# Hybrid attention and recurrence layer: a re-timed program begin (fewer filler products, x scaled by column halves, other banks for its transposes, three weights cast by POOL)

## The chip, the core and the metric

One core of a Trainium2 chip runs the whole program once. The metric is the device time of that run in microseconds (us). TensorE (PE) multiplies matrices into PSUM banks, VectorE (DVE), ScalarE (ACT) and GpSimd (POOL) do elementwise work, and SyncE (SP) issues nearly all transfers. Each engine executes its own list of instructions strictly in the order in which it was written; an instruction that waits for another engine holds up everything behind it in its list.

## The reference, cut to what matters

One layer over 2048 prompt frames and 64 sample frames of width 1024:

```python
def mixer_layer(x, ln_g, w_in, lb, norm_g, w_out, attn_fn, s0):
    aq, ak, av, ag, hq, hf, hi, hg = split(rms_norm(x, ln_g) @ w_in)     # 1024 -> 4096 columns
    o_a = attn_fn(aq, ak, av) * silu(ag)            # 8 heads x 64, chunks of 64, band of 576 keys
    o_b, S = hgrn2_branch(hq, hf, hi, hg, lb, norm_g, s0)                # 4 heads x 128
    y = x + concatenate([o_a, o_b]) @ w_out
    return y, k, v, S
# hgrn2: f = lb + (1 - lb) * sigmoid(hf), gated linear recurrence; final rms_norm on y
```

`lb` comes from a softmax over two rows of `lb_gamma`, computed once on the chip ("the forget bounds").

## The kernel before, in words

The 2112 frames are worked off in four super-blocks of 512, 576 (with the 64 sample frames), 512 and 512 columns. In each, `x` is normalised, transposed and multiplied with the 32 column tiles of `w_in` (projections j = 0 to 31 of that super-block); each projection feeds a recurrence head or a pair of attention heads. The output projection follows at the end.

**Products in three parts.** Every float32 operand is kept as a rounded part and a remainder (`xh` and `xl`, `w[:, 0]` and `w[:, 1]`), and a projection is 24 products into one accumulator bank: eight `xh` with the high weight, eight `xl` with the high weight, eight `xh` with the low weight. In the first super-block the weights come raw: one engine casts the high part (DVE, but POOL for j = 0), POOL subtracts four quarters to make the low part, and the pair is also written back for later super-blocks. Later super-blocks read the pairs back.

**One tile of x.** `x_tile` takes 128 rows of x: ACT squares and sums them (L369) and makes the reciprocal root mean square `rstd` (L337, L338); DVE multiplies the rows by `rstd` and the gain (L377); PE transposes eight 128x128 pieces, four per PSUM bank (L253); ACT casts each bank to `xh` (L403), and DVE subtracts to make `xl` (L407), which frees the bank. A super-block has two halves of two tiles (256 columns; in the second super-block the second half has a further tile of 64 rows). The projections j = 0 and j = 1 of a super-block, and its last two, go half by half, so that the next super-block's tiles can be made in between.

**Program begin.** SP issues the four x tiles and the first four weights; ACT's queue issues the gain row `gin`, `lbg` (the `lb_gamma` rows) and `gnorm`. PE first multiplies the identity with itself into a spare bank, which has no use for the result (`spinning`, L1953: the fillers), spreads the gain row over 128 partitions with two products whose weight has a single row (L1964), and then runs fillers until the planner lets the first transposes go. The forget bounds run behind the transposes of the second half.

**What sets the order.** A planner (`Plan`) in the host code writes out all lists: each piece of work is a generator that says when it wants to go on, by the planner's own clock `C.now` and assumed lengths; PE's list drives the clock. So a change of one length or wait at the start can move rows of every list further down.

Of the kernel before, what the change touches and what calls it, by code (L numbers as in the profile page):

```python
# [17 lines left out]
P = 128  # L18
D = 1024
# [164 lines left out]
def hymba_step(  # L184
# [105 lines left out]
    def forget_bounds():  # L290

        yield lambda: x_there.get((0, 1, 1), (0, 0))[0] == 4
        lmx = T(cst, [P, NHB], F32, "lmx")
        le = T(cst, [P, 2, NHB], F32, "le")
        dve.tensor_tensor(lmx, lbg[:, 0], lbg[:, 1], ALU.max)
        for i in range(2):
            dve.tensor_sub(le[:, i], lbg[:, i], lmx)
        t = C.dve(300)
        yield "A", t
        act.activation(le, le, AF.Exp)  # L300
        t = C.act(8, t)
        yield "D", t
        dve.tensor_add(lmx, le[:, 0], le[:, 1])
        dve.reciprocal(lmx, lmx)
        dve.tensor_mul(lb, le[:, 0], lmx)
        dve.tensor_scalar(oml, lb, -1.0, 1.0, ALU.mult, ALU.add)
        C.dve(400, t)
        have.add("bounds")
# [43 lines left out]
    def x_tile(sb, half, c, here=None, gain=None):  # L352
# [24 lines left out]
        dve.scalar_tensor_tensor(xn[:rows], xn[:rows], r[:rows], g, ALU.mult, ALU.mult)  # L377
        t = C.dve(1070, t)
        yield lambda: x_left.get((sb - 1, half), False)
        yield t  # L380
        ends = []
        for k0 in (0, 4):
            tags = ("g", "tr") if sb else ("acc", "tr", "g", "pv")
            while not any(tk[x].n for x in tags):
                some = [tk[x].when() for x in tags]
                yield min(some) if min(some) < NEVER else C.now + 150.0
            tag = [x for x in tags if tk[x].n][0]
            tk[tag].take()
            pt = psum(tag, bufs={"g": 1, "pv": 1}.get(tag, 2))
            for kt in range(k0, k0 + 4):  # L390
                transpose(pt[:, (kt - k0) * P : (kt - k0) * P + rows], xn[:rows, kt * P : (kt + 1) * P],
                          ident[:rows, :rows])
            ends.append((k0, tag, pt, C.pe()))
            if k0 and here is None:
                tk["xn"].put(1, C.pe())
            C.spawn(x_split(sb, half, c, rows, *ends[-1]), 0 if sb or half else -1)

    def x_split(sb, half, c, rows, k0, tag, pt, t):
# [6 lines left out]
        there(sb, half, 0, t)  # L405
# [4 lines left out]
        there(sb, half, 1, t)  # L410

    def there(sb, half, part, t):
        n, last = x_there.get((sb, half, part), (0, 0.0))
        x_there[sb, half, part] = (n + 1, max(last, t))
# [35 lines left out]
    def w_split(j, nt, raw, t, tok):  # L450
# [4 lines left out]
        if j == 0:  # L455
# [73 lines left out]
    def project(j, ranges, evac, close=True, ready=None):  # L529
# [3 lines left out]
        if ready:  # L533
            yield lambda: ready(0)
        for off, bn in ranges:
# [1366 lines left out]
    def program():  # L1902
# [55 lines left out]
        for _ in range(8):  # L1958
            spinning()
            C.now += 330.0  # L1960
# [7 lines left out]
        while tk["acc"].n == 2:  # L1968
            spinning()
            C.now += 224.0  # L1970
# [4 lines left out]
        for sb in range(nsb):  # L1975
# [6 lines left out]
            for u, (kind, g) in enumerate(JOBS[sb]):  # L1982
# [16 lines left out]
                if u in (1, len(JOBS[sb]) - 1):  # L1999
                    for half in range(2):  # L2000
                        yield from project(j - 1, [halves[half]], before, half == 1,
                                           lambda part: x_ready(sb, half, part))
                        yield from project(j, [halves[half]], evac, half == 1,
                                           lambda part: x_ready(sb, half, part))
# [154 lines left out]
```

## Time and profile before

| | |
|---|---|
| three runs | 1254.45, 1257.12, 1257.91 us; median 1257.12 |
| the profiled execution | 1256.82 us, span 1254.6 us (2.2 us lie around the span) |
| PE busy in the span | 1240.9 us (99%) |
| DVE, ACT, POOL busy | 894.6, 684.7, 415.2 us |
| mean granted TensorE clock | 0.996 |

The profile gives the busy time of each engine in any stretch, with the share of full speed that TensorE's clock was granted, lists instructions in order of time with the idle time ahead of them and what ended it, and sums waits by who was waited for. A bracket such as `[0.97 <-DVE xn L377]` is idle time of the engine just before that row, ended by the named instruction.

### The profile page before, as it was taken

Reading aid. Unit: us, or ns where it says so; the run is one execution under the profiler, and the core shown is the slowest. Engines: PE = TensorE matmul, PEld = TensorE weight load, DVE = VectorE, ACT = ScalarE, POOL = GpSimd, SP = SyncE. Lnnn points to the kernel's source line nnn. Section 1 sums busy time; section 2 is a strip of 40 time slices with the busy share of each in tenths; the row PEclk is TensorE's granted clock in tenths of the full one; section 3 lists DMA queues with packets and bytes.
Section 4 is the critical chain, followed back from the end, with each engine's and each line's share of the span. In section 5 each row is a group of like instructions: output and inputs, shape, how many; then the busy total and the mean of one; then the engine's idle time right before and its main releaser. Section 6 shows DMA issues by size and latency. Waiting matters only on the chain. (4 is left out here: it accounts for less than half of the span.)

```text
span 1254.6 us, 21417 instructions
## 1 busy us (share of the span) xinstructions
PE 1240.9 (99%) x7550; PEld 1093.7 (87%) x7550; DVE 894.6 (71%) x1887; ACT 684.7 (55%) x1533; POOL 415.2 (33%) x700
## 2 busy tenths in 40 slices
PE   8999999999999999999999999999999999999997
PEld 8888888999999999998888888988888888888786
DVE  6687879766867678687486667785857476867775
ACT  5354546654656556574465556665655445643443
POOL 6666665111120110201233242134241103474543
PEclk9999999999999999999999999999999999999999
DMA  8987779656555476655777878677666665987431
GB/s 334 311 306 248 279 285 370 212 158 228 178 189 159 145 223 216 193 166 172 252 266 240 299 255 281 227 248 251 219 244 202 222 219 197 342 275 241 136 125 67
DMA packets 137956, 287.94 MB, mean 230 GB/s; under 512 B 35257, under 2 KB 79289, under 8 KB 120186
## 3 DMA queue, kind: packets, MB, share of 16 engines
q1 hardware_dynamic: 137560, 286.58, 67.4%
q8 instruction: 59, 0.97, 0.3%
q14 instruction: 47, 0.39, 0.1%
q10 hardware_dynamic: 290, 0.01, 0.0%
HBM read 195.31 MB, written 92.27 MB: 229 GB/s over the span
## 5 line engine op out<-in xcount | busy, mean ns | idle before, releaser
L249 PE MATMUL acc<-xh,w 128*128 128x512 f32 (+2 forms) x2752 | 566.4, 345 | 0.7 <-ACT xh L403 0.4
L249 PEld LDWEIGHTS acc<-xh,w 128*128 128x128 f32 x2752 | 439.8, 189 | 50.4 <-issue 0.6
L249 PE MATMUL acc<-xl,w 128*128 128x512 f32 (+2 forms) x1376 | 293.4, 345 | 0.3 <-DVE xl L407 0.3
L249 PEld LDWEIGHTS acc<-xl,w 128*128 128x128 f32 x1376 | 220.2, 189 | 25.1 <-DVE xl L407 0.5
L928 ACT ACTIVATE pr<-pr,nm 128x640 f32<-128x640 f32 (+4 forms) x132 | 100.3, 760 | 59.7 <-DVE nm L911 58.8
L940 ACT CAST ph<-tr 128x512 fp32r<-128x512 f32 (+3 forms) x176 | 87.9, 507 | 74.1 <-PE pv L249 47.8
L464 POOL TENSOR_TENSOR w<-wraw,w 128x256 fp32r<-128x256 f32 x120 | 106.6, 914 | 56.9 <-DVE w L459 40.4
L943 DVE TENSOR_TENSOR ph<-tr,ph 128x512 fp32r<-128x512 f32 (+3 forms) x176 | 101.4, 588 | 27.6 <-ACT ph L940 26.8
L911 DVE CUSTOM_DVE_ANT_0 pr<-s,bias 128x640 f32<-128x640 f32 (+4 forms) x128 | 94.2, 736 | 34.8 <-PE s L249 34.1
L249 PE MATMUL pv<-ph,v 128*128 128x256 f32 (+2 forms) x344 | 97.8, 370 | 0.0
L253 PE MATMUL tr<-ident,pr 128*128 128x128 f32 x580 | 89.0, 273 | 1.4 <-DVE sig L634 0.6
L500 POOL TENSOR_TENSOR xn<-wraw,xn 128x256 fp32r<-128x256 f32 x48 | 39.4, 822 | 142.2 <-ACT xn L497 136.4
L982 DVE TENSOR_TENSOR mixa<-mixa,pv 64x256 f32<-64x256 f32 (+1 forms) x144 | 56.8, 395 | 36.0 <-ACT mixa L978 32.7
L1084 POOL TENSOR_TENSOR mixa<-mixa,sga 128x256 f32<-128x256 f32 (+1 forms) x36 | 29.1, 808 | 158.8 <-DVE mixa L982 146.3
L932 DVE TENSOR_SCALAR pr<-pr,sm 128x640 f32<-128x640 f32 (+4 forms) x132 | 76.9, 583 | 4.7
L253 PEld LDWEIGHTS tr<-ident,pr 128*128 128x128 f32 x580 | 69.9, 140 | 10.8 <-DVE sig L634 1.0
L1521 POOL TENSOR_TENSOR k<-ob 128x512 f32<-128x512 f32 (+2 forms) x20 | 18.2, 911 | 180.7 <-ACT ob L1512 161.9
L564 ACT ACTIVATE sig<-acc 128x512 f32<-128x512 f32 (+2 forms) x64 | 32.0, 499 | 64.8 <-PE acc L249 61.7
L249 PEld LDWEIGHTS pv<-ph,v 128*128 128x128 f32 (+1 forms) x344 | 58.4, 189 | 7.1
L978 ACT COPY mixa<-pv 64x256 f32<-64x256 f32 (+1 forms) x72 | 25.1, 349 | 62.3 <-PE pv L249 58.7
L249 PE MATMUL s<-kd,q 128*128 128x320 f32 (+2 forms) x232 | 56.5, 314 | 0.0
L249 PE MATMUL s<-kd,ql 128*128 128x320 f32 (+2 forms) x232 | 55.7, 310 | 0.0
(324 smaller groups left out, 2140.2 us busy)
## 6 DMA issues: line engine op xcount, KB each, us to landing
w<-wd SPq DMA_DIRECT2D x96, 1024.0 KB, 5.6
wd<-w SPq DMA_DIRECT2D x32, 1024.0 KB, 7.7
wraw<-in_w_in_dram SPq DMA_DIRECT2D x30, 512.0 KB, 5.6
wod<-xn SPq DMA_DIRECT2D x28, 512.0 KB, 5.4
xn<-in_x_prompt_dram SPq DMA_DIRECT2D x23, 512.0 KB, 4.6
bias<-biasd SPq DMA_DIRECT2D x24, 320.0 KB, 5.8
carry<-kd SPq DMA_DIRECT2D x12, 512.0 KB, 3.7
carry<-v SPq DMA_DIRECT2D x12, 512.0 KB, 6.7
```

Source lines behind the costliest of these rows:

```text
L249: pe.matmul(out, w, x, **kw)
L253: pe.transpose(out, x, idn)
L464: pool.tensor_sub(w[:, 1, k : k + 2], raw[:, k : k + 2], f32(w[:, 0, k : k + 2]))
L500: pool.tensor_sub(f32r(st[:, c.start + 512 : c.stop + 512]), src[:, c], st[:, c])
L564: act.activation(sig[:, :bn], acc, AF.Exp, scale=-1.0)
L911: dve.tensor_tensor_reduce(s[:, :nk].rearrange("p (a c) -> p a c", a=ns), sps[:, :ns, :kn], d.bias[:, h, bcol : bcol + nk].rearrange("p (a ...
L928: act.activation(s[:, :nk], s[:, :nk], AF.Exp, bias=nm[:, 0:1], scale=-1.0, accum_out=sm)
L932: dve.tensor_scalar(s[:, :nk], s[:, :nk], sm, None, ALU.mult)
L940: act.copy(ph[:krows, 0, :wid], pt[:krows, :wid])
L943: dve.tensor_sub(ph[:krows, 1, :wid], pt[:krows, :wid], f32(ph[:krows, 0, :wid]))
L982: dve.tensor_add(mix[hs, :qn], mix[hs, :qn], pv[hs, i, :qn])
L1084: pool.tensor_mul(mix[:, :n], mix[:, :n], d.sg[:, g0 : g0 + n])
```

## The change

Six edits, all in the planner's code:

1. Four fillers ahead of the gain products instead of eight, and three behind them instead of "until the first accumulator bank is taken".
2. In the first super-block DVE scales a tile of x in two column halves of 512, and the transposes of a half go as soon as that half is scaled.
3. The first super-block's transposes take banks `tr`, `pv`, `g` in this order of preference, no longer `acc`.
4. Projections that follow their x closely ask for each half of the 1024 features by itself (`x_ready` has a `k0`): the first four products of eight may go when the first half of the features is there.
5. The high parts of the weights j = 1 and j = 2 are cast by POOL too; j = 0 already was.
6. The forget bounds start as soon as the first `rstd` is planned (`r1`: the second tile's), no longer behind all transposes.

```diff
     def forget_bounds():
-        yield lambda: x_there.get((0, 1, 1), (0, 0))[0] == 4
...
         t = C.dve(300)
-        yield "A", t
+        yield lambda: "r1" in have
         act.activation(le, le, AF.Exp)
         t = C.act(8, t)
-        yield "D", t
+        yield lambda: "s1" in have
         dve.tensor_add(lmx, le[:, 0], le[:, 1])
...
         t = C.act(1700, t)
+        have.add(f"r{c // P}")
         if not sb:
             yield lambda: "gain" in have and (not half or x_there.get((0, 0, 1), (0, 0))[0] == 4)
-        yield "D", t
         g = g_in[:rows] if gain is None else gain
-        dve.scalar_tensor_tensor(xn[:rows], xn[:rows], r[:rows], g, ALU.mult, ALU.mult)
-        t = C.dve(1070, t)
-        yield lambda: x_left.get((sb - 1, half), False)
-        yield t
+        cut = (slice(0, 512), slice(512, D)) if not sb else (slice(0, D),)
         ends = []
         for k0 in (0, 4):
-            tags = ("g", "tr") if sb else ("acc", "tr", "g", "pv")
+            if k0 == 0 or not sb:
+                c_ = cut[k0 // 4]
+                yield "D", t
+                dve.scalar_tensor_tensor(xn[:rows, c_], xn[:rows, c_], r[:rows], g[:, c_], ALU.mult, ALU.mult)
+                t = C.dve(c_.stop - c_.start + 20, t)
+                if k0:
+                    have.add(f"s{c // P}")
+            yield lambda: x_left.get((sb - 1, half), False)
+            yield t
+            tags = ("g", "tr") if sb else ("tr", "pv", "g")
...
-    def x_ready(sb, half, part):
+    def x_ready(sb, half, part, k0):
         tiles = (SUPER[sb][3][half][1] + P - 1) // P
-        n, t = x_there.get((sb, half, part), (0, 0.0))
-        return n == 2 * tiles and t <= C.now
+        n, t = x_there.get((sb, half, part, k0), (0, 0.0))
+        return n == tiles and t <= C.now
...
-        if j == 0:
+        if j < 3:
             pool.tensor_copy(w[:, 0], raw)
             t = C.pool(700, t)
...
-                if ready and i == 1:
-                    yield lambda: ready(1)
                 if i == 2:
                     yield tl
                 for kt in range(KT):
+                    if ready and i < 2 and kt % 4 == 0:
+                        yield lambda: ready(i, kt)
                     mm(acc[:, :bn], w[:, wi, kt, :], x[:, kt, off : off + bn], bn,
...
-        for _ in range(8):
+        for _ in range(4):
             spinning()
-            C.now += 330.0
+            C.now += 400.0
             yield None
...
         have.add("gain")
-        while tk["acc"].n == 2:
+        for _ in range(3):
             spinning()
-            C.now += 224.0
+            C.now += 330.0
             yield None
         tk["g"].put()
```

PE's list at the program begin, before (`g` is the fillers' bank, `s` the spread gain, `xn` and `kd` hold x tiles; the two `acc` of rows four and five are x's transposes, the later ones are accumulators):

```order
L1953 MATMUL g_185<-ident_69 128x128 x8
L1964 MATMUL s_186<-gin_152,ones_74 128x512 x2
L1953 MATMUL g_185<-ident_69 128x128 x11
L253 MATMUL acc_223<-ident_69,xn_171 128x128 x4
L253 MATMUL acc_228<-ident_69,xn_171 128x128 x4
L253 MATMUL tr_240<-ident_69,xn_172 128x128 x4
L253 MATMUL tr_245<-ident_69,xn_172 128x128 x4
L249 MATMUL acc_266<-xh_153,w_219 128x256 x8
L249 MATMUL acc_266<-xl_154,w_219 128x256 x8
L249 MATMUL acc_266<-xh_153,w_219 128x256 x6
L253 MATMUL acc_305<-ident_69,xn_173 128x128 x4
L253 MATMUL tr_310<-ident_69,xn_173 128x128 x4
```

and now, from the third row of the list on (the first two are four fillers and the gain products):

```order
L1959 MATMUL g_185<-ident_69 128x128 x3
L253 MATMUL tr_215<-ident_69,xn_171 128x128 x4
L253 MATMUL tr_225<-ident_69,xn_171 128x128 x4
L253 MATMUL pv_231<-ident_69,xn_172 128x128 x4
L253 MATMUL tr_246<-ident_69,xn_172 128x128 x4
L249 MATMUL acc_252<-xh_153,w_221 128x256 x8
L249 MATMUL acc_252<-xl_154,w_221 128x256 x8
L249 MATMUL acc_252<-xh_153,w_221 128x256 x6
L253 MATMUL tr_300<-ident_69,xn_173 128x128 x4
L249 MATMUL acc_252<-xh_153,w_221 128x256 x2
L249 MATMUL acc_312<-xh_153,w_265 128x256 x6
L253 MATMUL tr_325<-ident_69,xn_173 128x128 x4
```

Nineteen fillers became seven, and the second half's transposes (`xn_173` and, further down, `kd`) now lie between the products of j = 0 and j = 1 of the first half, because a second accumulator bank is free for j = 1. DVE's list at the same place, now, from its third row on (before, it began with two scalings of 1024 columns and had the `lmx`, `le`, `lb`, `oml` rows behind the eighth `xl`):

```order
L294 TENSOR_TENSOR lmx_188<-lbg_83 128x4
L296 TENSOR_TENSOR le_189<-lbg_83,lmx_188 128x4 x2
L382 SCALAR_TENSOR_TENSOR xn_171<-xn_171,rstd_201,s_186 128x512 x2
L382 SCALAR_TENSOR_TENSOR xn_172<-xn_172,rstd_210,s_186 128x512
L412 TENSOR_TENSOR xl_154<-tr_215,xh_153 128x4x128
L382 SCALAR_TENSOR_TENSOR xn_172<-xn_172,rstd_210,s_186 128x512
L302 TENSOR_TENSOR lmx_188<-le_189 128x4
L303 RECIPROCAL lmx_188<-lmx_188 128x4
L304 TENSOR_TENSOR lb_81<-le_189,lmx_188 128x4
L305 TENSOR_SCALAR oml_82<-lb_81 128x4
L412 TENSOR_TENSOR xl_154<-tr_225,xh_153 128x4x128
L412 TENSOR_TENSOR xl_154<-pv_231,xh_153 128x4x128
```

The seven small operations of the forget bounds now stand ahead of and between the scalings and remainders on which the first projection waits. Behind the begin the lists differ in places for the first 740 of PE's 2682 rows, that is up to the second super-block, and only at two small places behind that. The place that the prediction speaks of is the passage from the first super-block to the second, where the last tile of x (64 rows, `xn_2741` before, `xn_2724` now) is transposed. PE's list there, before:

```order
L253 MATMUL g_2839<-ident_69,xn_2672 128x128 x4
L249 MATMUL acc_2836<-xh_153,w_2559 128x256 x6
L249 MATMUL s_2862<-kd_588,q_590 128x256
L249 MATMUL s_2862<-kd_588,ql_155 128x256
L249 MATMUL acc_2836<-xl_154,w_2559 128x256 x8
L249 MATMUL acc_2836<-xh_153,w_2559 128x256 x6
L249 MATMUL s_2886<-kd_588,q_590 128x384
L249 MATMUL s_2886<-kd_588,ql_155 128x384
L249 MATMUL acc_2836<-xh_153,w_2559 128x256 x2
L253 MATMUL g_2903<-ident_69,xn_2741 128x64 x4
L253 MATMUL tr_2908<-ident_69,xn_2741 128x64 x4
L253 MATMUL tr_2928<-ident_69,pr_2830 128x128
```

and now:

```order
L249 MATMUL acc_2832<-xh_153,w_2537 128x256 x8
L249 MATMUL s_2850<-kd_580,q_582 128x256
L249 MATMUL s_2850<-kd_580,ql_155 128x256
L249 MATMUL acc_2832<-xl_154,w_2537 128x256 x8
L249 MATMUL acc_2832<-xh_153,w_2537 128x256 x6
L249 MATMUL s_2879<-kd_580,q_582 128x384
L249 MATMUL s_2879<-kd_580,ql_155 128x384
L249 MATMUL acc_2832<-xh_153,w_2537 128x256 x2
L253 MATMUL g_2896<-ident_69,xn_2724 128x64 x4
L253 MATMUL tr_2901<-ident_69,xn_2724 128x64 x4
L249 MATMUL s_2914<-kd_580,q_582 128x512
L249 MATMUL s_2914<-kd_580,ql_155 128x512
```

Ahead of this piece stand the last transposes of the tile before (`xn_2658`, before `xn_2672`) and four products. Between those transposes and those of the 64-row tile there are now 28 projection products instead of 22, and the score products over 512 columns go ahead of the three transposes of `pr`, and no longer behind them. On ACT, the three activations that stood between the casts of the tile before and the square of the 64-row tile now stand behind that square, and the casts of the 64-row tile's `xh` now stand one activation later.

More of the change, by code (lines that the diff above doesn't have):

```diff
@@ L404, in x_split @@
         t = C.act(512, t)
-        there(sb, half, 0, t)
+        there(sb, half, k0, 0, t)
         yield "D", t
@@ L409, in x_split, with there @@
         tk[tag].put(1, t)
[L410 to L414, printed above, removed]
-    def x_ready(sb, half, part):
+        there(sb, half, k0, 1, t)
+    def there(sb, half, k0, part, t):
+        for key in ((sb, half, part), (sb, half, part, k0)):
+            n, last = x_there.get(key, (0, 0.0))
+            x_there[key] = (n + 1, max(last, t))
+    def x_ready(sb, half, part, k0):
         tiles = (SUPER[sb][3][half][1] + P - 1) // P
-        n, t = x_there.get((sb, half, part), (0, 0.0))
-        return n == 2 * tiles and t <= C.now
+        n, t = x_there.get((sb, half, part, k0), (0, 0.0))
+        return n == tiles and t <= C.now
     order = []
@@ L2001, in program @@
                         yield from project(j - 1, [halves[half]], before, half == 1,
-                                           lambda part: x_ready(sb, half, part))
+                                           lambda part, k0: x_ready(sb, half, part, k0))
                         yield from project(j, [halves[half]], evac, half == 1,
-                                           lambda part: x_ready(sb, half, part))
+                                           lambda part, k0: x_ready(sb, half, part, k0))
                         if u > 1:
```

2 lines of the change are left out of this document (1 added, 1 removed).

## The prediction

> **What bounds the kernel now.** I read the page's busy times, then the waits of PE, then busy time by stretches, and last the order of time at the two places that stand out.
>
> ```profile
> span 1254.6 us, 21417 instructions
> PE 1240.9 (99%) x7550; PEld 1093.7 (87%) x7550; DVE 894.6 (71%) x1887; ACT 684.7 (55%) x1533; POOL 415.2 (33%) x700
> ...
> PE g L1953 <- POOL one L279: 1.4, 1, 1.4
> PE g L253 <- DVE xn L377: 1.0, 1, 1.0
> PE tr L253 <- DVE kd L377: 0.9, 1, 0.9
> ```
>
> (Waits: who waited for whom, us in total, times, longest.) PE is busy all but 13.7 us of the span, so time is won only where PE waits, where its work has no use (the fillers), or where its clock is held back. The longest waits are at two places: the program begin (`one`, `kd`) and the passage to the second super-block (`g <- xn`). Stretches of 50 us, and stretches cut where the granted clock changes (the third figure from the end is that clock):
>
> ```profile
> 50.00:100.00 50.00, 50.00 (x272) 41.99 (x271) 38.15 (x78) 24.31 (x51) 31.19 (x46) 1.00 0.80 290
> 200.00:250.00 50.00, 48.56 (x353) 44.34 (x351) 41.45 (x86) 30.03 (x68) 17.36 (x32) 1.00 0.78 273
> ```
>
> ```profile
> 1.43:4.56 3.13, 3.13 (x14) 3.13 (x15) 0.74 (x2) 0.78 (x2) 1.52 (x6) 1.00 0.86 290
> 4.56:7.97 3.41, 3.41 (x18) 2.04 (x17) 0.99 (x1) 3.06 (x8) 0.58 (x1) 1.00 0.98 367
> 7.97:11.39 3.42, 3.42 (x18) 3.42 (x18) 1.48 (x2) 0.00 (x0) 3.25 (x5) 0.50 1.01 413
> 11.39:14.80 3.41, 2.71 (x23) 2.29 (x21) 2.55 (x5) 3.13 (x7) 0.58 (x1) 1.00 0.77 296
> 246.91:250.32 3.41, 1.84 (x15) 1.31 (x15) 2.95 (x9) 3.31 (x14) 0.00 (x0) 1.00 0.72 253
> 250.32:253.73 3.41, 3.41 (x12) 3.03 (x13) 3.37 (x13) 3.08 (x10) 0.43 (x3) 0.50 0.14 42
> ```
>
> Twice the clock is halved for 3.4 us: after a stretch of gain products and a few fillers (4.56 to 7.97), and after a stretch in which PE was busy for only 1.84 us (246.91 to 250.32). The begin on PE, in order of time:
>
> ```profile
> 1.43 3.53 PE L1953 MATMUL g<-ident 128*128 128x128 f32 x16 [1.43 <-POOL one L279]
> 4.89 1.98 PE L1964 MATMUL s<-gin,ones 1*128 1x512 f32 x4
> 6.80 4.03 PE L1953 MATMUL g<-ident 128*128 128x128 f32 x22
> 10.62 1.42 PE L253 MATMUL acc<-ident,xn 128*128 128x128 f32 x8
> 11.87 1.04 PE L253 MATMUL tr<-ident,xn 128*128 128x128 f32 x8
> 14.79 1.34 PE L249 MATMUL acc<-xl,w 128*128 128x256 f32 x8 [0.31 <-DVE xl L407]
> 15.97 0.88 PE L249 MATMUL acc<-xh,w 128*128 128x256 f32 x6
> 18.93 0.63 PE L253 MATMUL tr<-ident,kd 128*128 128x128 f32 x4 [0.87 <-DVE kd L377]
> 20.29 1.22 PE L249 MATMUL acc<-xh,w 128*128 128x256 f32 x8 [0.30 <-DVE xl L407]
> 28.10 2.96 PE L249 MATMUL acc<-xh,w 128*128 128x256 f32 x16
> ```
>
> The useful work up to the first 512-column product (half way through the last row, 29.1) is what counts: from 20.29 on it runs without a gap, 72 products of 0.12 us. From 15.97 PE still has 8 products of the first group, 16 transposes (0.11 each: eight back to back take 1.04 with the last one's latency) and 72 products: 0.96 + 1.75 + 8.64 = 11.35 us. It takes 13.1; so 1.75 us there are waits, and whatever moves the 15.97 forward comes on top.
>
> **The change part by part: the begin.** Eight fillers are 16 passes of 0.22 us; four fewer let the gain products go at 3.3 instead of 4.89.
>
> ```profile
> L1964 PEldq EVENT_SEMAPHORE  x1: 51/51/51, 2.2 to 2.2; - x1
> 6.98 2.47 DVE L377 SCALAR_TENSOR_TENSOR xn<-xn,rstd,s 128x1024 f32<-128x1024 f32 x2 [4.22 <-PE s L1964]
> 7.61 0.20 ACT L338 ACTIVATE rstd<-rstd 128x1 f32<-128x1 f32 x1
> L403 ACT CAST xh<-tr x4: 585/599/622, 12.6 to 19.6; 128x512 fp32r<-128x512 f32 x4
> 14.06 1.28 DVE L407 TENSOR_TENSOR xl<-tr,xh 128x512 fp32r<-128x512 f32 x2
> 22.64 0.58 DVE L303 TENSOR_TENSOR lmx<-le 128x4 f32<-128x4 f32 x1 [0.28 <-ACT le L300]
> 23.95 0.66 DVE L306 TENSOR_SCALAR oml<-lb 128x4 f32<-128x4 f32 x1
> ```
>
> The gain row is there: PE's sequencer had passed its semaphore at 2.2. But the fillers' 0.22 us a pass in the first stretch is the pace of the half-clock stretch (18 passes in 3.42), not that of a full clock (0.11), whatever the column says for it; the clock rose at 4.56, behind 3.13 us of fillers. Now that stretch holds 1.9 us of fillers and then gain products, whose single weight row did not keep the clock up between 4.56 and 7.97. I take the lower clock: four passes of 0.43 to 0.5 double to about 3.6 us and end at 7.0, as now. At full clock from 4.56 they would end at 5.9. The six filler passes behind them take 1.2 us (0.19 each), so PE is free at 8.3. DVE scales the first 512 columns in about 0.65 (half of 1.27) from 7.1, so they are there; the transposes go at 8.3 instead of 10.62.
>
> The 2.3 us do not reach the projection. In order: four transposes at half clock 1.1 us with their latency, 9.4; cast 0.6, 10.05; remainder 0.7, 10.8, which frees the bank for the fourth group; the fourth scaling to 11.4, for DVE has put it behind that remainder. Then the bounds' last four operations stand in DVE's list, 22.64 to 24.61 in the rows above: 2.0 us beside a busy POOL, as now. Three remainders of 0.6 follow: 15.3. Before, the last one of the first half ended at 15.34 (14.06 plus 1.28). So the first group's `xl` products end at 15.8 instead of 15.97 plus a little: 0.2 us won. At the full clock the same chain runs 1.5 us earlier (1.7 won).
>
> Behind it the 11.35 us of work remain, but the second half's pieces are now scaled in halves and lie between the products of j = 0 and j = 1, for which a second accumulator bank is free. What can still wait is the last remainder of `kd`: DVE has to do two scalings, `sig`, `gk` and the cast of the fourth weight ahead of it, which ends at 23.3 by the rows' lengths where PE wants it at 22.9. I count 0.6 us of waits instead of 1.75, so 1.1 won. **Begin: 0.2 + 1.1 = 1.3 us won** (2.8 at full clock; 0 as lower bound, if the remaining waits stay at 1.75).
>
> **The casts on POOL.** One costs 1.04 us there and 0.68 to 1.07 on DVE:
>
> ```profile
> 7.39 1.04 POOL L456 CAST w<-wraw 128x1024 fp32r<-128x1024 f32 x1 [4.05 <-DMA wraw<-in_w_in_dram]
> 14.22 2.82 POOL L464 TENSOR_TENSOR w<-wraw,w 128x256 fp32r<-128x256 f32 x4 [2.92 <-DVE w L459]
> L459 DVE CAST w<-kd x1: 1069/1069/1069, 16.5 to 16.5; 128x1024 fp32r<-128x1024 f32 x1
> ```
>
> POOL had 2.92 us idle waiting for DVE's cast; two casts fill 2.1 of it. Laid out by these lengths the third weight's low part is done at 24.4 and the fourth's at 27.4; PE asks for them after 16 products of 0.25 of each group, at 31.7 and 37.6. Price 0; the cover is 7 us. If it went, each us late would be one of PE's. The write-backs on SP stay behind the same subtractions and move with them. Asking per half of the features costs and saves nothing by itself: it only lets rows move.
>
> **The passage to the second super-block.**
>
> ```profile
> 243.89 0.60 PE L253 MATMUL g<-ident,xn 128*128 128x128 f32 x4
> 245.61 1.06 ACT L369 ACTIVATE ck<-xn 64x1024 bf16<-64x1024 f32 x1
> 248.68 0.46 PE L253 MATMUL g<-ident,xn 64*128 64x64 f32 x4 [0.97 <-DVE xn L377]
> 249.86 1.15 PE L253 MATMUL tr<-ident,pr 128*128 128x128 f32 x3 [0.47 <-DVE pr L932]
> 250.80 0.79 PE L249 MATMUL s<-kd,q 128*128 128x512 f32 x1
> 251.81 2.21 PE L249 MATMUL acc<-xh,w 128*128 128x320 f32 x8
> ```
>
> From 243.89 (the tile before) to 251.81 PE has 4.9 us of work at its usual pace and takes 7.9; the half clock until 253.73 costs another 1.0: 4.0 us lost. Now the three activations have left the path from cast to square, which is 0.6 + 1.06 + 0.9 + 1.28 (scaling) = 3.9 us, and PE has 28 products (3.3 us) and four score products (0.6): the wait of 1.0 goes. Late next is the score product over 512 columns: its bank comes free by DVE's maximum over the 384 columns, which stands behind the scaling, `v`, `sig` and `gk`: 1.0 us late. Then the casts of the 64-row tile, behind one more activation: 0.6 us. So 1.65 us of waits instead of 2.3, and the half clock comes or not: saved 2.3 without it, 0.6 with it (half of 3.41 us). The stretch holds about as little work as the one of 1.84 us that brought it on, so I lean to it: **1.2 us won**.
>
> **Sum.** 1256.82 - 1.3 - 1.2 = 1254.3; the median of the three runs is 0.3 higher, so 1254.6. I say 1254.5.
>
> [...]
>
> **The rivals.**
> *Full clock from 4.56.* 1.9 us of fillers suffice. For it: 1.84 us of mixed work is the only low case seen, the limit lies between that and the 2.71 of 11.39 to 14.80, which was not followed by a halved clock. Begin 2.8, passage 1.2 to 2.3: 4.0 to 5.1 us, 1252.2.
> *Nothing arrives.* The stretch 11.39 to 14.80 then holds only four transposes and eight products (1.4 us): like 246.91 it is followed by 3.4 us at half clock, in which PE has 3.4 us of demand and loses up to 1.7. Begin -0.4, passage 0.6: 1256.9. For it: that stretch has less work than the 2.71 us of now; against: PE waits in part of it anyway.
> *Slower.* The rows moved ahead of the second super-block meet DVE, which is busy 38 to 41 of 50 us there. A place where DVE is late by 1 us or more for a tile starves PE and halves the clock, as at 247: 4.0 us each. One such place more than now, with a begin of 0 to 1.3 and nothing won at the passage, gives 1259.8 to 1261.1, two give 1264; it decides from one wait of 1.5 us on. Against: the same planner made the order in which PE is now busy for 50.00 of 50 us from 50 to 100.
>
> **How the numbers follow.** Forecast 0.50, full clock 0.24, nothing arrives 0.14, slower 0.12. A measurement of this kernel tells about 0.3% (3.8 us) from no change: faster is below 1253.3, slower above 1260.9. Full clock is faster in nearly all its cases, the forecast in a sixth of its own (its two sizes at their upper ends together); slower is over the bound in two of three. Faster 0.23 + 0.08 = 0.31, slower 0.08, same the rest, 0.61. The range is 1251 to 1259; the forecast's own 1252.8 to 1256.4.
>
> **What would show it.** Right: first transposes near 8.3 and at half clock, the first 512-column product at 27 to 28 instead of 29.1, no wait of PE for `xn` at the passage but one for the 512-column scores there, and the rest of the program shifted as a whole. Wrong: gain products that end by 6 (full clock), a half clock between 14 and 18, or a new wait of PE over 1 us between 30 and 240.

## The result, and the profile after

| | before | now |
|---|---|---|
| median of six runs each | 1257.64 us (1254.45 to 1260.82) | 1253.63 us (1252.94 to 1254.63) |
| ratio | | 0.9966, interval 0.995 to 0.9983 |
| the profiled execution, its span | 1256.82, 1254.6 us | 1252.94, 1251.2 us |

The changed kernel is faster by 0.34%, just over the 0.3% that a measurement of this kernel can tell. Its runs lie within 1.7 us of each other, those of the kernel before within 6.4. The profile's page, and PE's waits (who waited for whom: us in total, times, longest):

```profile
span 1251.2 us, 21385 instructions
PE 1237.5 (99%) x7526; PEld 1089.1 (87%) x7526; DVE 888.8 (71%) x1889; ACT 684.5 (55%) x1533; POOL 412.4 (33%) x702
...
PE acc L249 <- DVE xl L412: 1.6, 2, 1.4
...
PE acc L249 <- ACT xh L408: 0.6, 2, 0.4
...
PE s L249 <- DVE nm L917: 0.4, 1, 0.4
```

The longest wait behind the start is now one for a remainder (`xl`), at the program begin. PE there, in order of time:

```profile
1.43 2.07 PE L1959 MATMUL g<-ident 128*128 128x128 f32 x8 [1.43 <-POOL one L279]
3.44 3.78 PE L1970 MATMUL s<-gin,ones 1*128 1x512 f32 x4
7.14 1.65 PE L1959 MATMUL g<-ident 128*128 128x128 f32 x6
8.58 1.91 PE L253 MATMUL tr<-ident,xn 128*128 128x128 f32 x8
...
15.23 1.34 PE L249 MATMUL acc<-xl,w 128*128 128x256 f32 x8 [1.39 <-DVE xl L412]
16.41 0.88 PE L249 MATMUL acc<-xh,w 128*128 128x256 f32 x6
...
23.78 0.74 PE L249 MATMUL acc<-xl,w 128*128 128x256 f32 x4 [0.20 <-DVE xl L412]
...
27.23 2.96 PE L249 MATMUL acc<-xh,w 128*128 128x256 f32 x16
```

The gain products end at 7.2, the transposes go at 8.58, and the first 512-column product (half way through the last row) comes at 28.2 instead of 29.1: 0.87 us won. Counted where both kernels have the same work behind them, that lead is still 0.85 at 180 us, 1.22 just ahead of the passage to the second super-block, 3.36 behind it and 3.35 at the last product. So the passage gave 2.1 us. Another 0.35 came between 180 and 225 us, where the rows stand in another order and PE waits for no more than 0.04 us in either kernel; every profile with the changed order has it, and why is open. The remaining half microsecond of the two execution times lies around the span (2.2 us before, 1.7 now). PE at the passage:

```profile
246.42 0.46 PE L253 MATMUL g<-ident,xn 64*128 64x64 f32 x4
...
247.56 0.50 PE L249 MATMUL s<-kd,q 128*128 128x512 f32 x1 [0.43 <-DVE nm L917]
...
249.21 1.44 PE L249 MATMUL acc<-xh,w 128*128 128x320 f32 x8 [0.35 <-ACT xh L408]
```

The wait for `xn` is gone, two smaller ones (0.43 and 0.35) have come, and the 320-column products run at full pace: eight in 1.44 us, where before they took 2.21. The records of the granted clock in the two traces begin and change at 4.56, 7.97, 11.39, 250.32, 253.73 and 1250.42 us in the kernel before, and at 10.75 and 1249.79 now: whole multiples of 3.413 us apart (1, 1, 70, 1 and 292 of them; 363). A window here is a stretch between two neighbouring points of that grid, laid out from the recorded changes. Three of the changed kernel's (columns: us, busy PE, PE's weight load, DVE, ACT, POOL, granted clock, share of the DMA engines, GB/s):

```profile
7.34:10.75 3.41, 3.41 (x17) 3.41 (x18) 2.50 (x4) 1.51 (x7) 3.27 (x5) 1.00 1.03 417
10.75:14.17 3.42, 2.22 (x15) 1.60 (x13) 3.32 (x7) 2.64 (x6) 3.42 (x5) 1.00 0.81 317
246.27:249.68 3.41, 2.62 (x18) 1.70 (x18) 3.06 (x12) 3.35 (x12) 0.00 (x0) 1.00 0.59 217
```

The trace records no halved clock between 10.75 and the last 1.4 us. The first record is the one at 10.75, so the 1.00 of the first row is no record but a default: by their pace (eight transposes in 1.91 us; they take 1.04 in the kernel before) the clock was still halved there.

### The profile page after: what moved, and what is told of

Read it like the earlier page. It is cut to its first block, busy times and chain, and to the rows that moved or that the text cites. A ratio compares the mean times of both kernels' runs of the same rounds, so it can differ in the third digit from the quotient of the medians.

```text
span 1251.2 us, 21385 instructions
## 1 busy us (share of the span) xinstructions
PE 1237.5 (99%) x7526; PEld 1089.1 (87%) x7526; DVE 888.8 (71%) x1889; ACT 684.5 (55%) x1533; POOL 412.4 (33%) x702
## 5 line engine op out<-in xcount | busy, mean ns | idle before, releaser
L470 POOL TENSOR_TENSOR w<-wraw,w 128x256 fp32r<-128x256 f32 x120 | 103.0, 886 | 55.1 <-DVE w L465 48.2
L988 DVE TENSOR_TENSOR mixa<-mixa,pv 64x256 f32<-64x256 f32 (+1 forms) x144 | 56.9, 395 | 35.5 <-ACT mixa L984 32.1
L570 ACT ACTIVATE sig<-acc 128x512 f32<-128x512 f32 (+2 forms) x64 | 32.1, 501 | 62.7 <-PE acc L249 59.9
```

Source lines behind the costliest of these rows:

```text
L470: pool.tensor_sub(w[:, 1, k : k + 2], raw[:, k : k + 2], f32(w[:, 0, k : k + 2]))
L570: act.activation(sig[:, :bn], acc, AF.Exp, scale=-1.0)
L988: dve.tensor_add(mix[hs, :qn], mix[hs, :qn], pv[hs, i, :qn])
```

## The experiments

The variants were measured in three turns, each beside the kernel before, whose median was 1257.4 to 1258.1 us. Ratios are to it; they are not the plain quotient of the medians.

**1. The fillers alone.** Edit 1 on the kernel before, nothing else:

```diff
-        for _ in range(8):
-            spinning()
-            C.now += 330.0
+        for _ in range(4):
+            spinning()
+            C.now += 400.0
...
-        while tk["acc"].n == 2:
-            spinning()
-            C.now += 224.0
+        for _ in range(3):
+            spinning()
+            C.now += 330.0
```

> The kernel before with edit 1 alone: four fillers ahead of the gain products, three behind; x scaled whole, transposes into the accumulator banks, casts on DVE, bounds late, and every list behind the begin as before. Theory A (the begin and the passage are two separate gains, the second made by the moved rows of the lists): the first transposes go near 8.6 us, the first 512-column product starts at about 27.8 (29.1 before), the passage keeps its wait for the 64-row tile and its half clock, total 1.0 to 1.5 us less than before. Theory B (the earlier begin makes both gains, because it shifts the passage against the clock's free-running windows): no half clock at the passage, total 3 us or more less than before.

Measured: 1261.52 us, ratio 1.0033 (1.0021 to 1.0045): slower. PE, ACT, and the clock's windows:

```profile
8.66 1.97 PE L253 MATMUL acc<-ident,xn 128*128 128x128 f32 x8
...
24.44 1.89 PE L249 MATMUL acc<-xh,w 128*128 128x256 f32 x8 [3.15 <-ACT sig L1237]
```

```profile
22.59 0.21 ACT L300 ACTIVATE le<-le 128x8 f32<-128x8 f32 x1 [2.56 <-DVE le L297]
...
24.03 0.37 ACT L1237 ACTIVATE sig<-acc 128x256 f32<-128x256 f32 x1
```

```profile
21.27:24.68 3.41, 0.26 (x3) 0.24 (x3) 2.83 (x7) 1.93 (x6) 2.56 (x4) 1.00 1.03 425
24.68:28.09 3.41, 3.41 (x18) 3.41 (x18) 1.40 (x3) 1.08 (x3) 0.00 (x0) 0.50 1.01 428
```

The transposes and the first products do come earlier. But in ACT's list the exponential of the forget bounds (`le`) stands ahead of all `sig`, and it waits for the bounds' first operations on DVE, which stand behind the eighth remainder. So the accumulator banks are not emptied, PE waits 3.15 us for one, and a window with 0.26 us of work is followed by one at half clock (0.50). First 512-column product: 31.8, 2.7 us later than before. By DVE's rows about half of that wait has a second source, which item 6 is about: the three first operations of the bounds, of four columns each, take 2.06 us here beside a busy POOL, and 0.42 in the kernel before (21.95 to 22.37):

```profile
20.50 0.70 DVE L295 TENSOR_TENSOR lmx<-lbg 128x4 f32<-128x4 f32 x1
21.23 1.33 DVE L297 TENSOR_TENSOR le<-lbg,lmx 128x4 f32<-128x4 f32 x2
```

An earlier start without earlier bounds only moves PE into a wait for the bounds.

**2. Fillers and bounds.** The same with edit 6 added in a shorter form: all of the bounds wait for the second tile's `rstd` (`r1`), and their last four operations not for the scaling (`s1`). Whole columns, the old banks and DVE's casts stay.

```diff
     def forget_bounds():
-        yield lambda: x_there.get((0, 1, 1), (0, 0))[0] == 4
+        yield lambda: "r1" in have
...
         t = C.act(1700, t)
+        have.add(f"r{c // P}")
```

> The kernel before with edits 1 and 6 alone: four and three fillers, and the forget bounds as soon as the second tile's `rstd` is planned. Whole columns, the old banks and DVE's casts stay. Theory A (edit 1 alone lost because ACT's exponential of the bounds stood ahead of the first `sig`, and PE waited 3.15 us for a bank behind it): that wait is gone, the first 512-column product comes at 26.8 to 27.8 instead of 29.1, and the time falls by 1 to 2 us against the kernel before, plus or minus what its different order does at the passage: 1253 to 1256.5. Theory B (edit 1 lost by its fewer fillers, that is by the clock): a half clock between 14 and 30, first 512-column product at 29 or later, 1258 to 1261.

Measured: 1253.29 us, ratio 0.9964 (0.9953 to 0.9975). The wait for `sig` is gone; the first 512-column product comes at 27.4:

```profile
8.66 1.97 PE L253 MATMUL acc<-ident,xn 128*128 128x128 f32 x8
...
13.68 1.33 PE L249 MATMUL acc<-xl,w 128*128 128x256 f32 x8
```

In the same turn the whole change measured 0.9961 (0.9949 to 0.9973; item 6). Two of the six edits give all of the gain that can be measured. That holds with the order that the planner makes behind them, in which PE has no wait at the passage either.

**3. The fillers back.** The changed kernel with all 19 fillers; the planner's clock, and with it every other row, as in the change.

```diff
         for _ in range(4):
             spinning()
+            spinning()
             C.now += 400.0
...
-        for _ in range(3):
-            spinning()
+        for n in (4, 4, 3):
+            for _ in range(n):
+                spinning()
             C.now += 330.0
```

> The changed kernel with all nineteen fillers back (eight ahead, eleven behind), no other row of any list different. Theory A: gain products from 4.9 to 6.9 at full clock, transposes near 10.6, first 512-column product near 30.0 (28.2 in the changed kernel), so the begin becomes about 1 us worse than before the change; the passage stays as in the changed kernel (no half clock): total 1.8 us more than the changed kernel, still 1.5 us less than before. Theory B: with the late begin the passage's half clock comes back and the total is at or above that of before.

Measured: 1256.05 us, ratio 0.9978 (0.9964 to 0.9992). The single runs fall apart: three at 1253.0 to 1253.95, seven at 1254.97 to 1257.5. The profiled one:

```profile
5.14 3.78 PE L1971 MATMUL s<-gin,ones 1*128 1x512 f32 x4
8.85 5.02 PE L1959 MATMUL g<-ident 128*128 128x128 f32 x22
```

The fillers run at half pace to 13.7, where the trace first records the full clock. The first 512-column product comes at 32.1, 3.9 us later than in the changed kernel, and all of that is left at the end; the passage keeps its gain. Between the medians lie 2.4 us, but the ratios of the two kernels differ by 0.12% (1.5 us) and their intervals overlap. By its single runs, twelve fillers more cost nothing in some executions and 4 us in others; where the clock's windows lie in those, only the profiled one shows.

**4. The passage, covered by other means.** The kernel before, with five products of the identity ahead of the 64-row tile's transposes:

```diff
+FILL = 5
...
+            if sb == 1 and rows < P and not k0:
+                for _ in range(FILL):
+                    pe.matmul(pt[:, :P], ident, ident, start=True, stop=True)
             for kt in range(k0, k0 + 4):
```

> The kernel before with five filler products (ten passes of 0.11 us, no use for the result) ahead of the 64-row tile's transposes at the passage, where PE waits 1.0 us. Nothing else differs. Theory A (the wait costs twice, the second time by the half clock that follows it): PE is busy for about 2.9 of 3.4 us in that stretch, no half clock follows, total 1.0 to 1.7 us less than before though PE does more. Rival D (the half clock is a mark in the record and costs little, the waits are the loss): total the same as before within 0.3 us.

Measured: 1257.59 us, ratio 1.0 (0.9987 to 1.0014).

```profile
1.42 3.79 PE L1957 MATMUL g<-ident 128*128 128x128 f32 x16 [1.42 <-POOL one L280]
5.14 3.78 PE L1968 MATMUL s<-gin,ones 1*128 1x512 f32 x4
...
250.57 1.28 PE L393 MATMUL g<-ident 128*128 128x128 f32 x10
251.78 0.46 PE L254 MATMUL g<-ident,xn 64*128 64x64 f32 x4
```

At the passage this execution is 1.3 us ahead of the kernel before: no halved clock; the wait for `xn` has become fillers of the same length. But its begin, the same rows as before, ran at half pace to 14.0 and was 2.9 us later (first 512-column product at 31.9). Of the two profiled executions with this begin, that of the kernel before, whose clock had risen at 4.56, is the early one. Filling the wait alone moves no median: its length is the same, and a halved clock can be saved only where there was one. In how many executions that is so, no run shows.

**5. The passage, undone.** The changed kernel with the square of the 64-row tile put back behind the three activations that make `sig` (`square` holds the lines and is called behind the next `sig`). On ACT four rows now stand ahead of the square, the three activations and a cast of `v` of 0.2 us, which did not stand there in the kernel before; no row of another engine changes its place.

```diff
...
-        act.activation(junk[:rows], xn[:rows], AF.Square, accum_out=ss[:rows])
-        r = rstd_of(ss, rows, D)
...
+        if sb == 1 and rows < P:
+            later.append(square)
+        else:
+            square()
...
+            if later:
+                later.pop()()
```

> The changed kernel with one thing put back at the passage: in ACT's list the three activations that make `sig` stand again ahead of the square of the 64-row tile, as before the change; every other engine's list is unchanged. Theory A (the passage's gain comes from the shorter path from the last cast to the scaling of the 64-row tile): the scaling, which ended at 246.1 in the changed kernel, ends 1.3 us later (0.38 + 0.51 + 0.42), PE waits about 1.0 us for `xn` again at 246.4, and everything behind moves by 1.0 us; in executions in which a clock window lies over that wait, 1.3 to 1.7 us of half clock come on top. Median 1254.6 to 1256. Theory B (what covers the 64-row tile is PE's own order, 28 products ahead of its transposes instead of 22): no wait for `xn`, the time of the changed kernel, 1253.6.

Measured: 1254.65 us, ratio 0.9978 (0.9966 to 0.999); five runs at 1253.1 to 1254.1, five at 1255.2 to 1255.7.

```profile
244.48 1.04 ACT L372 ACTIVATE ck<-xn 64x1024 bf16<-64x1024 f32 x1
...
246.21 1.27 DVE L393 SCALAR_TENSOR_TENSOR xn<-xn,rstd,gin 64x1024 f32<-64x1024 f32 x1 [1.59 <-ACT rstd L338]
...
247.54 0.46 PE L253 MATMUL g<-ident,xn 64*128 64x64 f32 x4 [1.12 <-DVE xn L393]
248.87 0.50 PE L249 MATMUL s<-kd,q 128*128 128x512 f32 x1 [0.62 <-DVE nm L928]
```

The wait is back (1.12), everything behind is 0.9 us later, and this execution had no halved clock. Three activations on ACT are what the 64-row tile had waited for. The trace shows this, and the time alone would not: the interval overlaps that of the change. The two groups of runs lie 1.9 us apart on average, about half of a window of 3.41; whether the upper five are those with a halved clock is not shown, since one of the runs was profiled.

**6. The begin's chain.** Five variants of the changed kernel ask what stands between the transposes and the first `xl` products. First the bounds' last four operations, moved on DVE behind the third scaling of the second half (`h3` is set there; no other row changes place):

```diff
         yield lambda: "s1" in have
+        t = C.dve(400, t)
+        yield lambda: "h3" in have
         dve.tensor_add(lmx, le[:, 0], le[:, 1])
...
-        C.dve(400, t)
...
-                if k0:
-                    have.add(f"s{c // P}")
+                have.add(f"{'hs'[k0 // 4]}{c // P}")
```

> The changed kernel with the last four operations of the forget bounds moved in DVE's list from ahead of the first half's remainders to behind the third scaling of the second half; no other row different. Theory A (DVE's list is what bounds the changed begin): the wait of 1.39 us ahead of the first xl product goes, the first 512-column product starts at about 26.7 instead of 28.2, total 1.2 to 1.6 us less than the changed kernel. Rival C (the half clock and the second half's scalings, which wait for ACT, bound the begin): at most 0.3 us less, the wait only moves to the second half.

Measured: 1252.66 us, ratio 0.9965 (0.9949 to 0.9981). The first `xl` products go at 13.9 instead of 15.2, but the last remainder of `kd` is then late by 0.7, and the first 512-column product comes at 27.7: 0.5 of 1.3 us arrive. Against the changed kernel's second profile (27.3, below) nothing is gained. Then the two casts back on DVE:

```diff
-            pool.tensor_copy(w[:, 0], raw)
+            (dve if j else pool).tensor_copy(w[:, 0], raw)
```

> The changed kernel with the high parts of weights j = 1 and j = 2 cast by DVE again, at the places in time where POOL casts them now; the rest of every list is unchanged. Theory A (price of POOL's casts 0, cover 7 us, and DVE has no room at the begin): DVE has 0.7 to 1.1 us more in front of the fourth remainder and again in front of the third tile's second scaling, so the last remainder of `kd` ends 1.4 us later than 23.7 and PE, which wants it at 23.8, waits 0.7 to 1.5 us more; first 512-column product at 28.9 to 29.7 instead of 28.2; median 1254.3 to 1255.2. Theory B (the casts lie in DVE's idle time either way): 28.2 and 1253.6.

Measured: 1252.35 us, ratio 0.996 (0.9947 to 0.9972), first 512-column product at 27.1. Both theories were wrong: DVE does two casts more and the begin is 1.1 us shorter than in the changed kernel's first profile. The reason stands in DVE's rows. In the changed kernel, with POOL's at the same time, first DVE, then POOL:

```profile
11.56 0.74 DVE L302 TENSOR_TENSOR lmx<-le 128x4 f32<-128x4 f32 x1
12.34 0.18 DVE L303 RECIPROCAL lmx<-lmx 128x4 f32<-128x4 f32 x1
12.55 0.45 DVE L304 TENSOR_TENSOR lb<-le,lmx 128x4 f32<-128x4 f32 x1
13.03 0.95 DVE L305 TENSOR_SCALAR oml<-lb 128x4 f32<-128x4 f32 x1
13.90 0.68 DVE L412 TENSOR_TENSOR xl<-tr,xh 128x512 fp32r<-128x512 f32 x1
```

```profile
11.56 1.42 POOL L470 TENSOR_TENSOR w<-wraw,w 128x256 fp32r<-128x256 f32 x2
12.93 1.04 POOL L462 CAST w<-kd 128x1024 fp32r<-128x1024 f32 x1
```

and with DVE's casts, where POOL is idle from 11.5 to 14.2:

```profile
11.56 0.15 DVE L302 TENSOR_TENSOR lmx<-le 128x4 f32<-128x4 f32 x1
...
12.16 0.17 DVE L305 TENSOR_SCALAR oml<-lb 128x4 f32<-128x4 f32 x1
12.24 0.68 DVE L412 TENSOR_TENSOR xl<-tr,xh 128x512 fp32r<-128x512 f32 x1
```

Four operations of four columns: 2.34 us from first start to the next row, or 0.68. Each slow one ends where an instruction of POOL ends (12.30, and the first of the two subtractions at about 12.3; 13.00 and 12.98; 13.98 and 13.97). To test it, the same kernel with two casts more on POOL, whose result POOL itself overwrites:

```diff
+            if j == 1:
+                pool.tensor_copy(w[:, 1], raw)
+                pool.tensor_copy(w[:, 1], raw)
```

> casts_pinned (DVE casts weights j = 1 and j = 2), with two more casts on POOL, 1.04 us each, where the changed kernel has POOL's cast of j = 1; they write the low part of that weight, which POOL overwrites behind them, so that nothing waits for their result, and the other engines' lists are those of casts_pinned. Theory A (a small DVE operation with both operands in SBUF cannot start while POOL is in the middle of an instruction): the bounds' four operations, 0.66 us in casts_pinned, take 1.5 to 2.5 us again, the next remainder ends that much later, and the first 512-column product is 0.5 to 1.5 us later than in casts_pinned (27.1); median 1252.8 to 1253.8. Theory B (what casts_pinned gains is something else, the order of POOL's subtractions or of DVE's rows): bounds 0.7 us, 27.1, 1252.4.

Measured: 1253.52 us, ratio 0.9967 (0.9954 to 0.998); first 512-column product at 28.2 again.

```profile
11.96 0.72 DVE L304 TENSOR_TENSOR lb<-le,lmx 128x4 f32<-128x4 f32 x1
12.71 0.67 DVE L305 TENSOR_SCALAR oml<-lb 128x4 f32<-128x4 f32 x1
```

```profile
11.62 1.04 POOL L465 CAST w<-wraw 128x1024 fp32r<-128x1024 f32 x1
12.62 0.73 POOL L473 TENSOR_TENSOR w<-wraw,w 128x256 fp32r<-128x256 f32 x1
```

Again the two end with POOL's instructions (12.68 and 12.66; 13.38 and 13.35). The bounds take 1.73 us, the 1.1 us are gone. It is POOL's work at that moment that costs, not DVE's.

The fillers behind the gain products left out, and that with either of the two others:

```diff
         for _ in range(3):
-            spinning()
             C.now += 330.0
```

> The changed kernel without the three fillers behind the gain products; all other lists unchanged. Theory A (the transposes count as work for the clock, and the three fillers only fill the time until the first scaling is done): the transposes go as soon as the first scaled columns are there, at about 8.0 instead of 8.58, the clock rises at the same time as now, the wait for the third remainder grows by as much as the transposes gain; first 512-column product 0 to 0.5 us earlier, median 1253.1 to 1253.7. Theory B (the fillers behind the gain make the window full that raises the clock): the clock rises a window of 3.4 us later, the transposes and the first products of j = 0 run at half pace for 3.4 us more, first 512-column product 1 to 2 us later, median 1254.6 to 1255.6.

> Both edits of bounds_pinned (the bounds' last four operations behind the third scaling of the second half) and nofill_behind (no fillers behind the gain products) on the changed kernel. If the two add up: first 512-column product at 27.2 to 27.7, median 1252.2 to 1252.7, the best so far. If the fillers are what raises the clock: 1253.6 to 1254.6.

> Both edits of casts_pinned (weights j = 1 and j = 2 cast by DVE) and of nofill_behind (no fillers behind the gain products) on the changed kernel. Each alone took 1.1 to 1.2 us from the first 512-column product (27.1 and 27.0 instead of 28.2). Theory A (both shorten the same chain, each by a piece of its own: the bounds' four operations take 0.7 instead of 2.4 us, the transposes go 0.4 us earlier): first 512-column product at 26.6 to 26.8, median 1251.8 to 1252.2, the best so far. Theory B (both only shift the bounds' operations against POOL's, and only one of the two can gain that): 27.0 and 1252.3 to 1252.7.

> The changed kernel once more, unchanged, on the same chip and in the same turns as the three others of this job, so that they can be set against it: median 1253.6, between 1252.9 and 1254.6.

| variant | first 512-column product | median | ratio, interval |
|---|---|---|---|
| no fillers behind | 27.0 | 1252.68 | 0.9966 (0.9955 to 0.9978) |
| bounds moved, no fillers behind | 27.5 | 1253.77 | 0.9975 (0.9963 to 0.9987) |
| DVE's casts, no fillers behind | 26.7 | 1253.16 | 0.9969 (0.9956 to 0.9981) |
| the changed kernel again | 27.3 | 1252.79 | 0.9961 (0.9949 to 0.9973) |

Without the fillers behind the gain the clock rises as early as with them: its first record is at 11.3, after a window that held transposes and some 0.6 us without work. The second profile of the unchanged changed kernel is 0.86 us earlier at its first 512-column product than the first, and the whole difference is the bounds: 1.48 us, from 11.56 to the next remainder at 13.04; POOL had started 0.13 us later (7.52 instead of 7.39), and its instructions lie otherwise against DVE's. Shorter begins don't show in the medians: the one with 26.7 has 1253.16, the one with 27.0 has 1252.68, and the changed kernel, with 28.2 and 27.3, has 1253.63 and 1252.79. A part of the reason lies far behind. ACT and PE late in the program, with DVE's casts and no fillers behind, and then in the changed kernel again:

```profile
1080.31 0.62 ACT L1682 CAST xh<-sig 128x512 fp32r<-128x512 f32 x1 [2.36 <-DMA sig<-mixd]
1085.73 0.41 PE L253 MATMUL tr<-ident,pr 128*128 128x128 f32 x2 [1.35 <-DVE ph L949]
```

```profile
1079.88 0.62 ACT L1682 CAST xh<-sig 128x512 fp32r<-128x512 f32 x1 [1.46 <-DMA sig<-mixd]
1085.30 0.41 PE L253 MATMUL tr<-ident,pr 128*128 128x128 f32 x2 [0.64 <-DVE ph L949]
```

ACT waits for a transfer, and PE for what stands behind it, by 0.46 to 1.4 us in the profiles of the changed kernel and its variants (0.26 in the kernel before). At the last product ahead of this wait the first of the two is 0.28 us ahead, and behind it 0.43 late: the wait takes 0.71. Whether the transfer comes late because of the earlier begin or by its own scatter is open. No variant is measurably faster than the change.

## Why the prediction was right, and where it was not

The time, 1253.63, lies in the range and 0.9 us under the forecast, inside the forecast's own range (1252.8 to 1256.4). The sign and the mechanisms were right; one term was mis-sized and one price was put in the wrong place. That the sum came so close is in part luck: the begin gave less than forecast, the passage more, 0.35 us came from a place that no term had, and half a microsecond lies around the span. The chances leaned to "within 0.3%". By the prediction's own bound, 1253.3, the median lies just inside; set against the six runs of the kernel before, it fell 0.04 of a percent beyond (the interval covers both sides).

**Gain products at half clock: right.** End 7.2 (forecast 7.0), four passes in 3.78 us (1.98 in the kernel before), transposes 8.58 (8.3), eight of them in 1.91 us. The six filler passes took 1.65 us instead of 1.2: the 0.19 us a pass was counted in a stretch that the fillers end at full clock. With it falls the rival of the full clock from 4.56, by which they would have ended at 5.9.

**The chain behind the transposes: right, a size off.** The first group's last remainder ends at 15.8 (forecast 15.3), so that the `xl` products stand 0.44 us later than before instead of 0.2 earlier. Most of the excess is the bounds: 2.34 us instead of the 2.0 counted. Item 6 shows that this number is no constant: 0.68, 1.48, 1.73 or 2.34, by POOL's instructions. The prediction had written "beside a busy POOL, as now" without asking what POOL does to them.

**The waits left: right.** From 16.41 to the first 512-column product 11.8 us for 11.35 of work: 0.45 of waits (forecast 0.6) instead of 1.75; 0.20 of it is a wait that the rows show. The begin gave 0.87 us (forecast 1.3; 1.73 in the second profile). By the prediction's sign, a first 512-column product at 27 to 28, the first profile (28.2) is 0.2 late and the second (27.3) fits.

**"The casts on POOL. Price 0": wrong in the place of the price.** The cover of 7 us for the weights held: no wait of PE for a `w` is in the list. But POOL's casts fill the time from 11.5 to 14.2 in which it otherwise stands idle and DVE's bounds run freely, and that was worth 1.1 us of the begin in the traces of item 6 (0.2 against the second profile of the changed kernel). In the medians it doesn't show.

**The passage: mechanism right, the term mis-sized.** Won 2.1 us, forecast 1.2, which lay between 2.3 without a halved clock and 0.6 with one; the case without came. The wait for `xn` went, by the three activations (item 5: 1.12 us with them put back); the next waits are those named, for the bank of the 512-column scores and for the casts of the 64-row tile, at 0.43 and 0.35 instead of 1.0 and 0.6. The shorter waits are worth 0.9 us by item 5, and the halved clock cost 1.3 us (item 4) where the prediction had counted 1.7. The step that failed: "The stretch holds about as little work as the one of 1.84 us that brought it on, so I lean to it." It holds 2.62. And less work than that went without a halved clock too, in the variant of item 1, at the same waits as the kernel before:

```profile
249.95:253.36 3.41, 2.14 (x20) 1.80 (x18) 2.98 (x8) 3.28 (x13) 0.00 (x0) 1.00 0.87 312
253.36:256.77 3.41, 3.07 (x17) 2.56 (x18) 3.34 (x14) 3.20 (x11) 0.00 (x0) 1.00 0.15 49
```

With 0.97 and 0.48 us of waits, split over two windows, the first holds 2.14 us of work, and the next is at full clock (1.00). In the kernel before both waits lie in one window, with 1.84. So by these two profiles its halved clock came with one execution's position of the windows, and the 1.3 us should have stood in the sum with a chance, for both kernels.

**The other rivals.** "Nothing arrives" rested on a halved clock behind the stretch with the first products: 10.75 to 14.17 holds 2.22 us, and the clock stayed. "Slower" needed a new wait of over 1 us in the first super-block: there is none between 30 and 240. A wait of that size did come in the variant of item 1, by another mechanism than the one named: the order of ACT's list.

**What no step had.** The profiled execution of the kernel before had its clock up at 4.56; in the other profile with the same begin, item 4, it rose at 14.01, and the same rows took 2.9 us longer. The changed kernel and its variants with seven fillers or fewer raised it between 10.7 and 12.4 in all nine of their profiles (items 1 and 2: 11.0 and 12.5); their gain products end at 7.2 each time. That the narrow spread of the new runs comes from this is argued from these profiles, not shown by a run.

## What to carry to other kernels

When the start of a chain is moved forward, look for what stands in the list of each engine behind it: here the fillers' removal alone made the kernel 0.33% slower, and eight small operations of another branch, moved with it, turned that into 0.36% faster. Before work is given to an idle POOL, look at what DVE does in that time, its tiny operations above all: here four of them took 0.68 us beside an idle POOL and 1.48 to 2.34 beside a busy one (item 6). Count a halved clock that follows one short wait as a chance and not as a fact of the kernel: here the same two waits fell into one window in one profile (1.84 us of work, then half clock) and into two in another (2.14 and 3.07, no half clock).

## What the runs showed of the hardware

**Small DVE operations ended with POOL's instructions.** An operation of four columns took 0.15 to 0.18 us beside an idle POOL, and up to 0.95 beside POOL's casts and subtractions (item 6); the reciprocal among them (0.18) and the remainders that read PSUM (0.68) were not stretched. The five slow ones of item 6 end within 0.03 us of the end of one of POOL's instructions. What sets them apart from those that were not stretched, no run shows. Nor is it settled which of POOL's instructions hold: in the kernel before, three such operations took 0.14 to 0.16 us during one of POOL's memsets (21.68 to 22.36), and a fourth 0.58 during the next.

**The clock's windows lie otherwise in each execution.** The same begin had the full clock from 4.56 in one execution and from 14.01 in another: 9.45 us later, which is 2.77 windows of 3.413. Counted from the span's start, the first point of the grid lies at 1.15 in the kernel before, 0.51 in the changed one, 0.79 in item 1 and 0.36 in item 4. In these profiles windows with 0.26 and 1.84 us of work were followed by one at half clock, windows with 2.14, 2.22 and 2.62 were not. Busy time alone does not settle it: in the kernel before, the window from 4.56 to 7.97 was busy throughout, for 1.98 us with the gain products, and half clock followed it as well.

**The clock rose behind a window of transposes alone.** Without any filler behind the gain products (`nofill_behind`), the clock's first record is at 11.3, in the middle of the transposes of the first half (8.1 to 12.0). The window ahead of it held twelve of them, 2.82 us of work, and nothing else. Their pace rises there: those twelve took 0.24 us each, the last four 0.63 together.
